# Reordering the queues of a pipelined cross-covariance attention: exponentials ahead of the V copy, doubling ahead of the output matmuls

## The chip, the cores and the metric

One NeuronCore of one Trainium2 chip. The metric is device time in microseconds (us) of the whole kernel; medians are over 3 to 7 runs, and smaller is better. A profile's span is about 1.8 us shorter than the time of the same run (153.7 against 155.51 before).

## The reference

For each of 8x12 heads, with 512 rows of 64 values:

```python
Q_norm = Q / (norm(Q, axis=-2) + 1e-10)          # each of the 64 columns over the 512 rows
K_norm = K / (norm(K, axis=-2) + 1e-10)
attn = einsum('bhnd,bhne->bhde', Q_norm, K_norm)  # 64 x 64 a head
attn = softmax(attn, axis=-1)
out  = einsum('bhnd,bhde->bhne', V, attn)
```

All arrays are float32. Q, K, V and the output are 12.58 MB each, 50.3 MB in all.

## The kernel before

A unit is four heads; there are 24 units. Each head has 32 partitions with 16 rows a partition. Work is spread over steps, so that in step s the Gram matrices of unit s run beside the output matmuls of unit s-3. The order of calls below is the order of instructions in every engine's queue.

```python
def grams(u):                       # TensorE, 64 matmuls
    for t in range(R):              # R = 16
        for h in range(HU):         # HU = 4
            x = qkb[u][NV * h:NV * (h + 1), t, :]      # 32 partitions x (Q 64 | K 64), bf16
            nc.tensor.matmul(gbuf[:, h, 0:2 * D], x, x, start=(t == 0), stop=(t == R - 1), tile_position=(NV * h, 0))
# keep_kq: ScalarE copies K'Q out of the Gram tile; norms: VectorE takes its diagonal, GpSimd ^-0.5
# scale_k: VectorE; logits: TensorE transposes K'Q, 4 f32 matmuls, 8 in the trace; scale_q: VectorE
def exps(u):
    nc.scalar.activation(ex[u], sl[u], AF.Exp)
# normalise: VectorE, sum, reciprocal, product to bf16, rows 0-63 of a
def vtrans(u):                      # TensorE, 8 transposes, then ScalarE
    for t in range(TP):
        nc.tensor.transpose(ps[:, t, :], vb[u][:, t, :], identb)
    nc.scalar.copy(vt[u], ps)

def outs(u, u2):                    # u = s-3, u2 = s-2
    p0 = half(0)                    # TensorE, 16 matmuls
    keep(0, p0)                     # ScalarE copies to so
    p1 = half(1)
    # doubling: rows 0-63 of a, to rows 64-127, by way of PSUM
    nc.tensor.matmul(dup[D:], identb[0:D, 0:D], a2[0:D, :, 0, :], tile_position=(0, D))
    nc.scalar.copy(a2[D:, :, 1, :], dup[D:])
    keep(1, p1)

ltile = ps_l.tile([128, 2, HU, D], F32, name="lgdup")   # one PSUM tile for both
lg, dup = ltile[0:D, 0], ltile[:, 1]
# ... cuts ...
for s in range(U + 3):
    on(load_qk, s + LOAD_AHEAD); on(load_v, s + V_AHEAD); on(store, s - STORE_LAG)
    on(exps, s - 2)
    on(cast_v, s - 2); on(cast_q, s + 1); on(normalise, s - 2); on(scale_k, s - 1)
    on(grams, s); on(keep_kq, s); on(norms, s); on(cast_k, s + 1)
    outs(s - 3, s - 2)
    on(logits, s - 1); on(scale_q, s - 1); on(vtrans, s - 2)
```

## Time and profile before

| | before |
|---|---|
| time, median of the first 3 runs | 153.58 us (152.27 to 154.35) |
| span of the profiled run | 153.7 us (its time 155.51, about 1% above the median) |
| mean granted TensorE clock | 0.769 |
| first and last V cast (vb) on ScalarE | 16.79 and 144.26 us |
| step (kq copy to kq copy) at full / low clock (granted 1.00 and 0.61 in these two) | 5.03 / 5.87 us |

Main rows are shown in the prediction below. A line of the timeline: start, duration, engine, what, and in brackets the idle time before it and its cause.

```profile
q8 instruction: 21, 0.34, 0.9%
```

```profile
PEld L150 <- issue: 6.6, 16, 1.4
```

### The profile page before, as it was taken

Reading aid. Unit: us, or ns where it says so; the run is one execution under the profiler, and the core shown is the slowest. Engines: PE = TensorE matmul, PEld = TensorE weight load, DVE = VectorE, ACT = ScalarE, POOL = GpSimd, SP = SyncE. Lnnn points to the kernel's source line nnn. Section 1 sums busy time; section 2 is a strip of 40 time slices with the busy share of each in tenths; the row PEclk is TensorE's granted clock in tenths of the full one; section 3 lists DMA queues with packets and bytes.
Section 4 is the critical chain, followed back from the end, with each engine's and each line's share of the span. In section 5 each row is a group of like instructions: output and inputs, shape, how many; then the busy total and the mean of one; then the engine's idle time right before and its main releaser. Section 6 shows DMA issues by size and latency. Waiting matters only on the chain.

```text
span 153.7 us, 6358 instructions
## 1 busy us (share of the span) xinstructions
PE 106.8 (69%) x2712; PEld 85.8 (56%) x2712; DVE 95.5 (62%) x360; ACT 101.0 (66%) x169; POOL 43.8 (29%) x35
## 2 busy tenths in 40 slices
PE   0437498768896668759659876958879975947640
PEld 0436386557675557538548754837666853825430
DVE  0378567776767865975876687576686597353300
ACT  3002465985777686796777588567768579677770
POOL 6043045035224405304422512430431531320000
PEclk9999999995569776895985589596855599585555
DMA  4999999999999999999999999999985703321333
GB/s 190 321 402 417 410 408 406 403 414 407 417 411 413 416 410 417 410 415 417 408 419 411 418 419 410 421 413 378 390 320 189 270 4 136 141 82 59 136 136 136
DMA packets 13851, 50.73 MB, mean 330 GB/s; under 512 B 1536, under 2 KB 1536, under 8 KB 13824
## 3 DMA queue, kind: packets, MB, share of 16 engines
q1 hardware_dynamic: 13824, 50.34, 82.5%
q8 instruction: 21, 0.34, 0.9%
q14 instruction: 6, 0.05, 0.1%
HBM read 37.75 MB, written 12.58 MB: 327 GB/s over the span
## 4 chain that ended last, share of the span: by engine, by line
PE 38%; ACT 33%; issue 14%; DMA 8%; SPq 2%; DVE 1%; ACTq 1%
PE lgdup L116 14%; PE vps L138 12%; ACT vb L81 8%; DMA vf<-in_V_dram 8%; ACT so L157 8%; PE gram L88 7%; ACT ab L168 6%; ACT kq L93 5%; PE po L150 4%; ACT ex L124 4%; ACT vt L140 3%; SPq L63 1%; SPq L62 1%; PE lgdup L167 1%; DVE ab L132 1%
## 5 line engine op out<-in xcount | busy, mean ns | idle before, releaser
L105 POOL TENSOR_TENSOR rq<-nsq,mhalf 128x4 f32<-128x4 f32 x24 | 41.4, 1725 | 93.0 <-DVE nsq L100 93.0
L88 PE MATMUL gram<-qkb 32*128 32x128 bf16 x1536 | 40.1, 282 | 9.4 <-DVE qkb L77 9.4
L140 ACT COPY vt<-vps 128x1024 bf16<-128x1024 bf16 x24 | 24.3, 1012 | 29.6 <-PE vps L138 29.6
L88 PEld LDWEIGHTS <-qkb 32*128 32x128 bf16 x1536 | 34.6, 127 | 13.3 <-DVE qkb L77 9.8
L116 PE MATMUL lgdup<-ident,kqs 64*64 64x64 f32 x192 | 22.0, 276 | 19.8 <-ACT ab L168 19.8
L116 PEld LDWEIGHTS lgdup<-ident,kqs 64*64 64x64 f32 x192 | 17.9, 179 | 30.1 <-ACT ab L168 29.9
L157 ACT COPY so<-po 128x512 f32<-128x512 f32 x48 | 28.0, 585 | 1.8 <-PE po L150 0.7
L128 DVE TENSOR_REDUCE esum<-ex 64x4 f32<-64x256 f32 x24 | 9.9, 411 | 28.0 <-ACT ex L124 28.0
L81 ACT CAST vb<-vf 128x1024 bf16<-128x1024 f32 x24 | 24.8, 1032 | 1.8 <-DMA vf<-in_V_dram 1.8
L150 PE MATMUL po<-ab,vt 128*32 128x128 bf16 x768 | 20.4, 259 | 7.9 <-ACT vt L140 4.1
L100 DVE CUSTOM_DVE_ANT_0 scr<-gram,ident 128x128 f32<-128x128 f32 x96 | 22.2, 287 | 3.1 <-ACT kq L93 2.5
L150 PEld LDWEIGHTS <-vt 128*32 128x32 bf16 x768 | 14.8, 116 | 13.2 <-issue 6.6
L138 PE MATMUL vps<-identb,vb 128*128 128x128 bf16 x192 | 21.5, 280 | 0.0
L74 DVE CAST qkb<-qf 128x1024 bf16<-128x1024 f32 x24 | 16.3, 677 | 6.6 <-DMA qf<-in_Q_dram 6.6
L138 PEld LDWEIGHTS <-vb 128*128 128x128 bf16 x192 | 16.0, 127 | 2.9 <-ACT vb L81 0.6
L77 DVE CAST qkb<-kf 128x1024 bf16<-128x1024 f32 x24 | 16.5, 689 | 0.5 <-DMA kf<-in_K_dram 0.5
L120 DVE TENSOR_TENSOR sl<-lgdup,rq 64x256 f32<-64x256 f32 x24 | 10.0, 417 | 9.2 <-PE lgdup L116 9.0
L93 ACT COPY kq<-gram 64x256 f32<-64x256 f32 x24 | 8.8, 367 | 10.4 <-PE gram L88 9.8
L124 ACT ACTIVATE ex<-sl 64x256 f32<-64x256 f32 x24 | 10.0, 415 | 1.9 <-DVE sl L120 1.9
L167 PE MATMUL lgdup<-ab,identb 64*64 64x256 bf16 x24 | 7.5, 314 | 5.1 <-DVE ab L132 4.7
L110 DVE TENSOR_TENSOR kqs<-kq,rq 64x256 f32<-64x256 f32 x24 | 10.1, 423 | 0.8
L132 DVE TENSOR_TENSOR ab<-ex,rinv 64x256 bf16<-64x256 f32 x24 | 10.0, 417 | 0.8
(14 smaller groups left out, 27.5 us busy)
## 6 DMA issues: line engine op xcount, KB each, us to landing
qf<-in_Q_dram SPq DMA_DIRECT2D x24, 512.0 KB, 10.1
kf<-in_K_dram SPq DMA_DIRECT2D x24, 512.0 KB, 10.0
vf<-in_V_dram SPq DMA_DIRECT2D x24, 512.0 KB, 10.1
out_dram<-so SPq DMA_DIRECT2D x24, 512.0 KB, 9.9
```

The source lines that it names most:

```text
L74: nc.vector.tensor_copy(qkb[u][:, :, 0:D], qf[u])
L77: nc.vector.tensor_copy(qkb[u][:, :, D:], kf[u])
L81: nc.scalar.copy(w.rearrange("p t d -> p (t d)"), vf[u])
L88: nc.tensor.matmul(gbuf[:, h, 0:2 * D], x, x, start=(t == 0), stop=(t == R - 1), tile_position=(NV * h, 0))
L93: nc.scalar.copy(kq[u][D:], gbuf[D:, :, 0:D])
L100: nc.vector.tensor_tensor_reduce(out=scr, in0=gbuf[:, h, 0:2 * D], in1=ident, scale=1.0, scalar=1e-20, op0=ALU.mult, op1=ALU.add, accum_ou ...
L105: nc.gpsimd.tensor_tensor(out=r, in0=n2, in1=mhalf, op=ALU.pow)
L116: nc.tensor.matmul(lg[:, h, :], kqs[u][D:, h, :], ident[D:, D:], tile_position=(D, 0))
L138: nc.tensor.transpose(ps[:, t, :], vb[u][:, t, :], identb)
L140: nc.scalar.copy(w, ps)
L150: nc.tensor.matmul(po[rows, k, :], vt[u][:, TP // 2 * i + k, rows], a[:, h].rearrange("p a d -> p (a d)"), tile_position=(0, NV * h),)
L157: nc.scalar.copy(so[u][:, TP // 2 * i:TP // 2 * (i + 1), :], po)
```

## The change

Intent: ScalarE takes the exponentials while TensorE transposes V, rather than after copying the transposed V, and the doubling copy goes ahead of the output copies, so that the logits, which waited 29.9 us for that copy in the profile before, wait less.

```diff
-    def outs(u, u2):
-        def half(i): ...
-        def keep(i, po): ...
-        if 0 <= u < U:
-            p0 = half(0); keep(0, p0); p1 = half(1)
-        if 0 <= u2 < U:
-            nc.tensor.matmul(dup[D:], identb[0:D, 0:D], a2[0:D, :, 0, :], tile_position=(0, D))
-            nc.scalar.copy(a2[D:, :, 1, :], dup[D:])
-        if 0 <= u < U:
-            keep(1, p1)
+    def doubled(u):
+        nc.tensor.matmul(dup[D:], identb[0:D, 0:D], a[0:D, :, 0, :], tile_position=(0, D))
+        nc.scalar.copy(a[D:, :, 1, :], dup[D:])
+    def outs(u):
+        for i in range(2): ...            # 16 matmuls, then the copy to so
@@ the loop over steps
-        on(exps, s - 2)
         on(cast_v, s - 2)
@@
-        outs(s - 3, s - 2)
+        on(doubled, s - 2)
+        on(outs, s - 3)
         on(logits, s - 1)
         on(scale_q, s - 1)
+        on(exps, s - 1)
         on(vtrans, s - 2)
```

(Shortened; the statements on each side are the same, in another order.)

## The prediction

> **What bounds the kernel now.** I read the page's busy shares and DMA row first, then the waits, then the timeline of two whole steps. The kernel runs 27 pipelined steps over 24 units of four heads; step s works on the Gram matrices of unit s, the logits of s-1, the softmax, doubling and V transposes of s-2, and the output matmuls of s-3.

> ```profile
> PE 106.8 (69%) x2712; PEld 85.8 (56%) x2712; DVE 95.5 (62%) x360; ACT 101.0 (66%) x169; POOL 43.8 (29%) x35
> DMA  4999999999999999999999999999985703321333
> ```

> No engine is full. The DMA row is full for the first three quarters, which looks like a memory bound but is not: it is the loads running ahead. The waits say so:

> ```profile
> PEld lgdup L116 <- ACT ab L168: 29.9, 23, 2.2
> ACT vt L140 <- PE vps L138: 29.6, 23, 2.2
> DVE esum L128 <- ACT ex L124: 28.0, 23, 1.9
> ACT vb L81 <- DMA vf<-in_V_dram: 1.8, 1, 1.8
> ```

> After the first unit no compute engine waits for V. Instead, 23 times each, the logits matmuls wait for ScalarE's doubling copy, ScalarE then waits for the V transposes, and VectorE waits for the exponentials: a ring. One turn at full TensorE clock, from one keep of kq to the next:

> ```profile
> 62.34 0.37 ACT L93 COPY kq<-gram 64x256 f32<-64x256 f32 x1
> 62.74 0.59 ACT L157 COPY so<-po 128x512 f32<-128x512 f32 x1
> 62.97 0.29 DVE L100 CUSTOM_DVE_ANT_0 scr<-gram,ident 128x128 f32<-128x128 f32 x1
> 63.35 0.37 ACT L168 CAST ab<-lgdup 64x256 bf16<-64x256 f32 x1
> 63.77 0.68 PE L116 MATMUL lgdup<-ident,kqs 64*64 64x64 f32 x8 [0.95 <-ACT ab L168]
> 63.82 0.69 DVE L77 CAST qkb<-kf 128x1024 bf16<-128x1024 f32 x1
> 64.37 0.62 PE L138 MATMUL vps<-identb,vb 128*128 128x128 bf16 x8
> 64.55 0.42 DVE L120 TENSOR_TENSOR sl<-lgdup,rq 64x256 f32<-64x256 f32 x1
> 65.08 1.01 ACT L140 COPY vt<-vps 128x1024 bf16<-128x1024 bf16 x1 [0.76 <-PE vps L138]
> 65.99 0.41 ACT L124 ACTIVATE ex<-sl 64x256 f32<-64x256 f32 x1
> 66.31 1.03 ACT L81 CAST vb<-vf 128x1024 bf16<-128x1024 f32 x1
> 67.37 0.37 ACT L93 COPY kq<-gram 64x256 f32<-64x256 f32 x1
> ```

> Start to start: kq 0.40, first so 0.61, ab to logits 0.42, logits 0.60, transposes to vt 0.71, vt 0.91, ex 0.32, vb 1.06: 5.03 us. Note that sl is done at 64.97 and ex starts only at 65.99. At the low clock the same ring takes 5.87 us (the kq copies at 78.05 and 83.92), with TensorE as follows:

> ```profile
> 83.30 1.05 PE L150 MATMUL po<-ab,vt 128*32 128x128 bf16 x32
> 84.28 0.42 PE L167 MATMUL lgdup<-ab,identb 64*64 64x256 bf16 x1
> 85.34 1.11 PE L116 MATMUL lgdup<-ident,kqs 64*64 64x64 f32 x8 [0.65 <-ACT ab L168]
> 86.39 1.04 PE L138 MATMUL vps<-identb,vb 128*128 128x128 bf16 x8
> 87.36 1.89 PE L88 MATMUL gram<-qkb 32*128 32x128 bf16 x64
> 89.17 0.79 PE L150 MATMUL po<-ab,vt 128*32 128x128 bf16 x32
> ```

> [...] ex had its input 1.02 us early and sat behind vt. [...] logits (in the bank's lower half) start 0.05 us after the doubling copy of its upper half ends, and in the step at 18 us, where VectorE was free, the norms start 0.03 us after kq ends, though both only read the Gram tile. [...] its clock row reads 9 in the first 30 us, where logits take the slow 1.11 us, so I go by durations. [...] The trace has one table load, 1.28 us, in the whole run, with copies and Exp alternating; their new order adds none.

> **The change part by part.** No instruction is added or removed; counts and shapes stay. Only queue order moves.

> a) Doubling ahead of the outputs. ScalarE's order becomes vb, kq, ab, so, so, ex, vt. The first so leaves the stretch between kq and ab: 0.61 us off the way to the logits, both clocks.

> b) Exponentials ahead of vt. ScalarE no longer waits for the transposes with nothing to do but runs ex in that gap; ex no longer waits for vt, so the softmax of VectorE starts earlier. VectorE's 28.0 us of waiting for ex should nearly vanish.

> c) The new ring. With K the start of kq: ab may start at K+0.39, logits at about K+0.80, done K+1.45 at full clock. VectorE[...] starts the norms at K+0.40; they take 0.85 (62.97 to 63.82), the K cast 0.73 (63.82 to 64.55), so sl starts at K+1.98, after the logits. Then sl to ex 0.44 (14.08 to 14.52 in the first unit, where ex waited for sl alone), ex 0.32, vt 0.91, vb 1.06. Sum 0.40+0.85+0.73+0.44+0.32+0.91+1.06 = 4.71 us. The transposes end at K+2.1 and vt starts at K+2.74, so they are hidden; both so copies end at about K+2.0, before ex at K+2.42. ScalarE's own work, start to start, is 0.91+0.32+1.06+0.39+0.39+0.61+0.60 = 4.28, so it would still idle 0.4. The normalised attention is ready at about K+4.1, the doubling matmul and the outputs end by K+5.0, that is 0.3 into the next step, before its logits at 0.8. So full-clock step: 4.71 against 5.03.

> d) At the low clock, TensorE itself: logits 1.05, transposes 0.97, Gram 1.81 (all start to start above), outputs 0.98 (83.30 to 84.28), doubling an estimated 0.4: 5.2 us. Its idle 0.65 goes, because ab is now copied while the outputs run. So low-clock step: 5.2 against 5.87.

> e) Mix. The timeline puts the first vb at 16.8 and the last at 144.3, 23 steps, 5.54 us each. The profiled time is 155.5 for a span of 153.7, 1.8 more, so the timed 153.58 is a span of 151.8 and a step of (151.8-16.8-9.4)/23 = 5.46, with 9.4 us from the last vb to the end. That is half way between 5.03 and 5.87: half of the steps slow. Keeping half: (4.71+5.2)/2 = 4.96 us. The beginning waits for loads and the final vb-to-store tail has the same ScalarE queue, so both stay. Span 16.8+23x4.96+9.4 = 140.3, time 142.

> **Rivals.** *Transfers take over.* V of unit u is preceded by 8+3u transfers, later four a step. The rows give 413 GB/s, so 1.27 us for 0.524 MB: V of unit 20 lands at 16.8+6x3.8+14x5.1 = 111 us. My vb of unit 20 is at 16.8+20x4.96 = 116, so loads stay 5 us ahead. Were every step at full clock, it would be 111: the loads meet compute, and the time is at best about 136 (16.8+23x4.71+9.4+1.8). For it: the full DMA row. Against: loads now lead by several steps.
> *TensorE takes over altogether.* A denser TensorE could spend all its steps at the slow clock: 16.8+23x5.2+9.4+1.8 = 147.6. For it: 93% busy from 80 to 90 us at clock 0.52. [...]
> *A new wait takes the place.* The doubling matmul, now ahead of the outputs, needs VectorE's attention; if that came late it would block outputs, so copies and logits behind it. Against: I find about 0.5 us of slack (outputs ending at 0.3, logits due at 0.8). Were a quarter to half of the gain lost so, 145 to 148.

> **Range and chances.** The prediction is 142 us, 7.5% less. The range 137.5 to 146.5 runs from nearly all steps at the full clock to nearly all at the slow one, or a lost third. Over 2% faster needs under 150.5: even the slow-clock rival and the half-lost gain pass, so 0.95; within 2% 0.04; slower 0.01, since nothing is added.

> **What would show it right or wrong.** Right: between kq copies 4.7 us where transposes take 0.62, 5.2 where they take 1.04; ex starting 0.03 us after sl; vt starting straight after ex; VectorE's wait for ex and TensorE's wait for ab each under a third; VectorE's norms starting on kq's end. Engine busy times should be unchanged but for TensorE's clock. Wrong: V loads named as what vb waits for (transfers); doubling matmul waiting long for ab from VectorE, with so copies waiting for po (the new wait); slow durations in nearly every step (clock).

The marked cuts are statements on the hardware that no trace here shows. Part c's norms at K+0.40 rest on the one step at 18 us in which they started 0.03 us after kq ended. What "full" and "low" clock stand for, in the profile before: transposes of 0.62 us in the step from 62.34 us, at a granted clock of 1.00, and of 1.04 us at 86.39, in a stretch (80 to 90 us) at 0.52.

## More of the kernel before

TensorE has 64 Gram, 32 output, 8 logits, 8 transposing and 1 doubling matmuls a step, each with a weight load: 226 instructions.

```profile
57.34 0.24 PE L150 MATMUL po<-ab,vt 128*32 128x128 bf16 x4 [1.16 <-issue]
```

The queue that the profile names "instruction" moved 0.34 MB in 21 packets, 16 KB each: the program's own instructions come by DMA. TensorE once stood for 1.16 us in the middle of the output matmuls, waiting for no semaphore that the profile shows ("issue").

## The result, and the profile after

The changed kernel takes 146.46 us (median of 4 runs, 145.65 to 147.19) against 153.77 us for the one before in its 4 runs. The ratio is 0.9537 (95% interval 0.9452 to 0.9623). Ratios here are the mean time of one kernel's fast runs over that of the other's fast runs of the same rounds, so not quite the ratio of the medians. That is faster by 4.6%, where 7.5% was predicted: the direction and the ring were right, the size was not.

First the page's busy and DMA rows, then waits (total us, times, longest).

```profile
PE 105.3 (73%) x2712; PEld 83.4 (58%) x2712; DVE 93.1 (64%) x360; ACT 99.0 (68%) x169; POOL 38.9 (27%) x35
DMA  4999999999999999999999999999999963312333
```

```profile
DVE scr L100 <- ACT kq L93: 22.6, 23, 2.2
PEld L88 <- issue: 12.3, 18, 2.2
PE gram L88 <- issue: 8.9, 9, 2.0
PEld lgdup L116 <- ACT ab L146: 4.0, 7, 0.8
DVE esum L128 <- ACT ex L124: 1.4, 3, 0.5
```

VectorE's wait for the exponentials fell from 28.0 to 1.4 us and the weight load's wait for the doubling copy from 29.9 to 4.0, as intended. The norms now wait for the kq copy, as the new ring has it. ScalarE still loads its table once, for 1.28 us. But the matmuls and weight loads of the Gram matrices now stand idle for "issue", which names no engine.

A full-clock step of the timeline (granted clock 1.00), to hold against the one in the prediction:

```profile
63.26 0.37 ACT L93 COPY kq<-gram 64x256 f32<-64x256 f32 x1
63.66 0.29 DVE L100 CUSTOM_DVE_ANT_0 scr<-gram,ident 128x128 f32<-128x128 f32 x1 [0.68 <-ACT kq L93]
64.51 0.69 DVE L77 CAST qkb<-kf 128x1024 bf16<-128x1024 f32 x1
65.11 0.41 DVE L120 TENSOR_TENSOR sl<-lgdup,rq 64x256 f32<-64x256 f32 x1
65.56 0.42 ACT L124 ACTIVATE ex<-sl 64x256 f32<-64x256 f32 x1 [0.56 <-DVE sl L120]
65.88 0.99 ACT L140 COPY vt<-vps 128x1024 bf16<-128x1024 bf16 x1
66.77 1.04 ACT L81 CAST vb<-vf 128x1024 bf16<-128x1024 f32 x1
67.84 0.37 ACT L93 COPY kq<-gram 64x256 f32<-64x256 f32 x1
```

Start to start: 0.40 + 0.85 + 0.60 + 0.45 + 0.32 + 0.89 + 1.07 = 4.58 us. It is the predicted ring, link by link; ex starts 0.04 us after sl ends and vt follows it at once.

A stretch at low clock (granted 0.50) after the loads had ended (no stall in it, TensorE only):

```profile
121.86 1.05 PE L156 MATMUL po<-ab,vt 128*32 128x128 bf16 x32
122.83 1.11 PE L116 MATMUL lgdup<-ident,kqs 64*64 64x64 f32 x8
123.88 1.03 PE L138 MATMUL vps<-identb,vb 128*128 128x128 bf16 x8
124.85 1.89 PE L88 MATMUL gram<-qkb 32*128 32x128 bf16 x64
126.67 0.42 PE L145 MATMUL lgdup<-ab,identb 64*64 64x256 bf16 x1
127.02 1.05 PE L156 MATMUL po<-ab,vt 128*32 128x128 bf16 x32
```

127.02 - 121.86 = 5.16 us, with TensorE never idle: the 5.2 of the prediction.

So 4.58 and 5.16 both came out as predicted, or better. Yet 14 steps in the loaded stage (kq of unit 5 at 30.44 us to unit 19 at 106.67) took 5.445 us each, more than either. The profile names no wait for it, only these stalls:

```profile
66.19 0.96 PE L88 MATMUL gram<-qkb 32*128 32x128 bf16 x56 [0.64 <-issue]
72.35 0.79 PE L88 MATMUL gram<-qkb 32*128 32x128 bf16 x42 [2.01 <-issue]
78.37 0.93 PE L88 MATMUL gram<-qkb 32*128 32x128 bf16 x27 [1.24 <-issue]
```

(A stall of 0.24 us, ending at 84.39, is left out here.)

```profile
90.41 0.63 PE L156 MATMUL po<-ab,vt 128*32 128x128 bf16 x31 [1.28 <-issue]
96.70 0.44 PE L156 MATMUL po<-ab,vt 128*32 128x128 bf16 x17 [1.46 <-issue]
```

Two things give them away. They end every 6.0 to 6.3 us (66.19, 72.35, 78.37, 84.39, 90.41, 96.70), at different places of the program. And the counts between two of them are nearly fixed, as a view of one stretch shows. Its columns are the length, then the busy time of TensorE's matmuls, its weight loads, VectorE, ScalarE and GpSimd (instructions in brackets), the granted clock, the share of the DMA engines and GB/s:

```profile
66.20:72.30 6.10, 3.51 (x127) 2.66 (x128) 5.06 (x19) 5.49 (x9) 1.43 (x1) 1.00 1.03 413
```

TensorE ran 127 + 128 = 255 instructions, with one of the 226-instruction steps ending inside. The granted clock was 1.00 here, so a low clock does not explain these 6.10 us. Counted from end to end of these six stalls, it ran 256, 256, 257, 259 and 258 matmuls and weight loads, at granted clocks from 0.52 to 1.00. So I take the instructions to come in blocks of 256. The queue fits: its packets have 16 KB each, and they start at 63.6, 69.9, 75.9, 82.0 and 88.0 us, some 2.5 us ahead of the ends of the stalls (66.19 to 90.41). The n-th packet started when TensorE had run about 256 x n instructions (272 at the first, 2706 at the tenth). That these are TensorE's blocks shows in their number: it has 24 x 226 = 5424 instructions, 21 whole blocks of 256; with 218 a step the queue has 20 packets, with 162 it has 15, with 154 it has 14, each time the whole blocks in TensorE's count.

Where the 9.1 us between the two spans (153.7, 144.6) came from, as differences of the same marks: the first vb 2.1 us earlier (16.79 to 14.72), first vb to kq of unit 5 1.2, the 14 loaded steps 2.2, kq of unit 19 to the last vb 3.5, the end 0.1. Only 2.2 us of it comes from 14 of the steps. The first mark is mostly luck of the start: in the versions below, the split one aside, it lies anywhere from 15.0 to 17.6. The profile before is of a run about 1% slow, at nearly the same clock (0.769, against 0.767), so I lean on step lengths and not on the difference of the spans.

### The profile page after: what moved, and what is told of

Read it like the earlier page. It is cut to its first block, busy times and chain, and to the rows that moved or that the text cites. A ratio compares the mean times of both kernels' runs of the same rounds, so it can differ in the third digit from the quotient of the medians.

```text
span 144.6 us, 6358 instructions
## 1 busy us (share of the span) xinstructions
PE 105.3 (73%) x2712; PEld 83.4 (58%) x2712; DVE 93.1 (64%) x360; ACT 99.0 (68%) x169; POOL 38.9 (27%) x35
## 4 chain that ended last, share of the span: by engine, by line
PE 56%; DVE 14%; issue 14%; ACT 9%; DMA 3%; ACTq 0%; SPq 0%; DVEq 0%
PE gram L88 23%; PE lgdup L116 11%; PE po L156 10%; PE vps L138 9%; DVE scr L100 6%; PE lgdup L145 4%; DVE qkb L77 4%; DMA kf<-in_K_dram 3%; ACT vb L81 3%; ACT kq L93 2%; ACT vt L140 2%; DVE sl L120 1%; DVE qkb L74 1%; ACT so L160 1%; DVE ab L132 1%
## 5 line engine op out<-in xcount | busy, mean ns | idle before, releaser
L105 POOL TENSOR_TENSOR rq<-nsq,mhalf 128x4 f32<-128x4 f32 x24 | 36.5, 1520 | 89.9 <-DVE nsq L100 89.9
L88 PE MATMUL gram<-qkb 32*128 32x128 bf16 x1536 | 39.7, 270 | 18.7 <-DVE qkb L77 9.3
L88 PEld LDWEIGHTS <-qkb 32*128 32x128 bf16 x1536 | 32.4, 121 | 24.2 <-issue 12.3
L100 DVE CUSTOM_DVE_ANT_0 scr<-gram,ident 128x128 f32<-128x128 f32 x96 | 22.2, 288 | 22.7 <-ACT kq L93 22.6
L160 ACT COPY so<-po 128x512 f32<-128x512 f32 x48 | 26.0, 589 | 6.4 <-PE po L156 5.2
L156 PE MATMUL po<-ab,vt 128*32 128x128 bf16 x768 | 21.1, 264 | 7.5 <-issue 6.3
L81 ACT CAST vb<-vf 128x1024 bf16<-128x1024 f32 x24 | 25.1, 1045 | 0.0
L140 ACT COPY vt<-vps 128x1024 bf16<-128x1024 bf16 x24 | 24.0, 1001 | 1.2 <-PE vps L138 0.4
L116 PE MATMUL lgdup<-ident,kqs 64*64 64x64 f32 x192 | 22.3, 279 | 2.6 <-ACT ab L146 2.5
L124 ACT ACTIVATE ex<-sl 64x256 f32<-64x256 f32 x24 | 10.0, 417 | 18.7 <-DVE sl L120 18.7
L116 PEld LDWEIGHTS lgdup<-ident,kqs 64*64 64x64 f32 x192 | 18.4, 184 | 6.7 <-ACT ab L146 4.0
L138 PE MATMUL vps<-identb,vb 128*128 128x128 bf16 x192 | 20.4, 269 | 0.1
L93 ACT COPY kq<-gram 64x256 f32<-64x256 f32 x24 | 8.8, 368 | 14.4 <-PE gram L88 13.9
L77 DVE CAST qkb<-kf 128x1024 bf16<-128x1024 f32 x24 | 16.5, 689 | 0.5 <-DMA kf<-in_K_dram 0.5
L138 PEld LDWEIGHTS <-vb 128*128 128x128 bf16 x192 | 14.8, 121 | 2.7 <-issue 0.6
L120 DVE TENSOR_TENSOR sl<-lgdup,rq 64x256 f32<-64x256 f32 x24 | 9.9, 414 | 9.9 <-PE lgdup L116 8.6
L145 PE MATMUL lgdup<-ab,identb 64*64 64x256 bf16 x24 | 8.2, 342 | 5.7 <-DVE ab L132 5.6
L128 DVE TENSOR_REDUCE esum<-ex 64x4 f32<-64x256 f32 x24 | 9.7, 405 | 1.4 <-ACT ex L124 1.4
```

The source lines that it names most:

```text
L77: nc.vector.tensor_copy(qkb[u][:, :, D:], kf[u])
L81: nc.scalar.copy(w.rearrange("p t d -> p (t d)"), vf[u])
L100: nc.vector.tensor_tensor_reduce(out=scr, in0=gbuf[:, h, 0:2 * D], in1=ident, scale=1.0, scalar=1e-20, op0=ALU.mult, op1=ALU.add, accum_ou ...
L105: nc.gpsimd.tensor_tensor(out=r, in0=n2, in1=mhalf, op=ALU.pow)
L116: nc.tensor.matmul(lg[:, h, :], kqs[u][D:, h, :], ident[D:, D:], tile_position=(D, 0))
L140: nc.scalar.copy(w, ps)
```

## The experiments

All times below are medians of fast runs; the kernel before took 152.37, 153.16 and 153.33 us in the three batches. Every version is correct unless it is said not to be.

### Each half of the change alone

```diff
# exps_only: outs(u, u2) as before
-        on(exps, s - 2)
         on(scale_q, s - 1)
+        on(exps, s - 1)
# dup_only: doubled and outs as after
+        on(exps, s - 2)                # first in the step, as before
-        on(exps, s - 1)
```

> Only the exponentials move; doubling and outputs stay as before. Theory F (TensorE's instructions arrive in blocks of 256 at one block per about 6.15 us while the transfers are full, so a step of 226 instructions takes no less than 226/256 x 6.15 = 5.4 us): the ring without the fetch would be about 4.8 us at full clock, still under 5.4, so the loaded stage stays at 5.4 us a step and only the stage after the loads gains a little less: 147 to 149. Theory C (no fetch limit; the low-clock step is simply 5.6 us of TensorE work): the doubling copy again stands between kq and the logits, TensorE idles again, 150 to 152.

> Only the doubling moves; the exponentials still stand behind the V copy. Ring by the durations of before: 4.45 us at full clock and about 5.2 at low clock, both under 5.4. Theory F: same as the whole change, 145.5 to 148. Theory C: the exponentials still start late, so half of the gain or less, 149 to 151.

Measured: exps_only 150.01 us (ratio 0.9867, interval 0.9774 to 0.9961), dup_only 151.21 (0.9948, 0.9854 to 1.0042). Both totals lie at the edges of C's ranges and above F's, so by the totals this did not go F's way. By stages it did: the loaded steps are 5.445 and 5.509 us, against 5.445 with both moves and 5.605 before. Three different orders, nearly one step. (The profile of dup_only is of its fastest run, 149.67 us at clock 0.821; its other four took 151.03 to 151.25.) They differ where the loads do not press: from unit 19 to 23 5.15 us a step for exps_only, 4.57 for dup_only and 5.08 for both. At full clock a step without a stall is 4.94 us for exps_only and 4.57 for dup_only, so there the doubling move alone already has the 4.58 of both. At low clock the doubling move alone is no faster than the kernel before: its steps without a stall reach 5.92 us (75.71 to 81.63 at clock 0.50) where about 5.2 was expected, against 5.87. The two single moves also started 1.3 to 1.7 us later than the whole change (first vb at 16.41 and 16.03, against 14.72). Neither alone gives the gain; the totals cannot be split into a share for each.

### No loads after the fifth unit

```diff
 def load_qk(u):
+    if u >= 5:
+        qf[u], kf[u] = qf[u - 5], kf[u - 5]
+        return
# likewise load_v; wrong results on purpose; same compute instructions
```

> The changed kernel with Q, K and V loaded for the first five units only and reused for the rest (wrong results on purpose); all compute instructions unchanged. Theory F: with the transfers idle the blocks come fast, the TensorE stalls named issue vanish, steps are 4.6 at full clock and about 5.2 at low clock: 136 to 141, blocks less than 5.7 us apart. Theory C: nothing of TensorE's work changed, 145 to 147.

> The kernel before, likewise with loads for five units only (wrong results on purpose). Theory F: its own ring of 5.03 and 5.87 us is mostly slower than the fetch, so it gains little, 0 to 3 us: 151 to 154, and the distance between the two kernels without loads is 11 us or more in place of 7. Theory C: both unchanged, distance 7 us.

Measured: the changed kernel 133.43 us (ratio 0.8787, 0.8718 to 0.8856), the kernel before 149.56 (0.9845, 0.9749 to 0.9940), below its expected 151. Rival C falls: no TensorE work changed, and 13 us went. The reordering is worth 149.56 - 133.43 = 16.1 us without loads, and 7 with them. The DMA row of the changed kernel without loads:

```profile
DMA  4999995404422430342244044213403421432133
```

The instruction counts are those of the page after (2712 matmuls and as many weight loads), and the DMA engines are at less than half from about 27 us on. No matmul stalls on "issue" any more, blocks come unevenly and mostly sooner (4.3 to 7.5 us apart, 5.3 on average, where less than 5.7 was expected of all), and the loaded-stage step is 4.582, the ring exactly. This is better than predicted (136 to 141), and the mean granted clock was 0.877 in place of 0.767. In the new order the versions without stalls have the higher clock (0.844 to 0.877 in their profiles, against 0.767). The old order without loads has no stall over 0.25 us either, and its fast runs stay at 0.771 to 0.776, so there the clock did not rise without stalls; what raises it was not tested apart.

### Fewer TensorE instructions, all loads kept

```diff
# after_gram256: wrong results on purpose, the same number of columns streamed
-        for t in range(R):
+        for t in range(0, R, 2):
-                nc.tensor.matmul(gbuf[:, h, 0:2 * D], x, x, ...)
+                y = qkb[u][NV * h:NV * (h + 1), t:t + 2, :].rearrange("p a d -> p (a d)")
+                nc.tensor.matmul(gbuf[:, h, 0:4 * D], x, y, ...)
# after_k64: correct; each head on 64 partitions for Q and K
+    Q2, K2 = (... "(u g p f) -> u p g f", p=128, g=2 ...)
-                x = qkb[u][NV * h:NV * (h + 1), t, :]                   # 16 x 4 matmuls of 32 rows
+                x = qkb[u][D * q:D * (q + 1), R // 2 * g + t, :]        # 8 x 2 x 2 matmuls of 64 rows
# after_bf16lg: correct
-        kqs: F32, transposed against ident
+        kqs: BF16, transposed against identb          # 16 instructions become 8
```

> The changed kernel, all loads kept, but the Gram matmuls taken in pairs: 32 of 256 columns in place of 64 of 128 (same columns streamed, cross terms wrong on purpose), so TensorE has 162 instructions a step in place of 226. Theory F: 162/256 x 6.15 = 3.9 us, no longer a bound; the ring's 4.6 us and the full transfers (5.1 us a step) are: 134 to 140, no TensorE stalls named issue over 0.5 us. Rival T (loads slow the engines in some other way, say by memory contention, and the number of instructions does not matter): 144 to 147.

> A correct kernel with as few TensorE instructions as the one above: Q and K are laid out with 64 partitions a head (two rows of 2 KB a partition), so a Gram matrix takes 8 matmuls of 64 rows in place of 16 of 32 rows, 162 instructions a step. Theory F: 134 to 141, if 2 KB rows do not slow the transfers. Rival T: 144 to 148.

> The changed kernel with the logits' transposing matmuls in bf16: 4 matmuls and 4 weight loads a step in place of 8 and 8, 218 instructions a step. Theory F: 218/256 x 6.15 = 5.24 us a step in the loaded stage in place of 5.43, some 16 steps: 3 us less, 143 to 145. Rival T: shorter TensorE work at the low clock only, 145 to 147.

Measured: after_gram256 135.86 us (ratio 0.8895, 0.8816 to 0.8973), after_k64 138.60 (0.9093, 0.9004 to 0.9182), after_bf16lg 141.21 (0.9282, 0.9180 to 0.9384). Rival T falls: the loads are all there, the DMA row stays full, and yet 8 to 11 us go with the 64 instructions, and 5 with eight. The step of the loaded stage fits the count: 218 instructions give 5.227 us, where 218/256 x 6.15 is 5.24. By time, after_bf16lg did 2 us better than expected. The 14 loaded steps gave 14 x (5.445 - 5.227) = 3.1 us, as expected; most of the rest came after them, from the kq copy of unit 19 to the last vb (26.1 us in place of 28.6), which the expectation left out.

At 162 instructions another bound shows. The DMA row and a wait of after_k64:

```profile
DMA  4999999999999999999999999999999999984233
```

```profile
ACT vb L83 <- DMA vf<-in_V_dram: 5.7, 9, 2.0
```

The engines keep to 4.58 us a step until about 67 us, then wait for V and take 5.1: at last the loads themselves. This is the rival "transfers take over" of the prediction, with the 5.1 us a step that it worked out; its best time for that, about 136 us, is near the 135.86 and 138.60 measured.

### The layout under the old order, and the instructions put back

```diff
# before_k64: the layout of after_k64 in the kernel before
# after_k64_tiny: after_k64 with 32 matmuls of one column ahead of each unit's Gram sums
+        for i in range(8):
+            for g in range(2):
+                for q in range(2):
+                    x = qkb[u][D * q:D * (q + 1), R // 2 * g + i, :]
+                    nc.tensor.matmul(gbuf[:, 2 * g + q, 511:512], x, x[:, 0:1], start=True, stop=True, ...)
```

> The kernel before with the 64-partition layout, 162 TensorE instructions a step. Theory F: the fetch no longer binds, but its own ring of 5.03 and 5.87 us does, so it gains no more than it did without loads: 149 to 151, and the change of order is worth 10 to 13 us at this instruction count in place of 7 at 226. If the layout itself were what is faster, it would gain as much as the changed kernel did (8 us): 145 to 146.

> The 64-partition version with 32 matmuls of one column added ahead of the Gram sums (results not used), so 226 TensorE instructions a step again with little work in them. Theory F: the loaded stage goes back to 226/256 x 6.15 = 5.4 us a step with stalls named issue: 143 to 148. If the work and not the number counts: 32 short matmuls fit into TensorE's idle time at full clock, 138 to 141.

Measured: before_k64 147.54 us (ratio 0.9605, 0.9528 to 0.9682), after_k64_tiny 150.03 (0.9773, 0.9696 to 0.9850).

The old order gains some 6 us from the layout, more than the 2 to 4 expected, and not quite the 8 of the changed kernel. Its steps are its own ring, 5.03 and 5.87 (in the profile of a slow run, 151.78 us), with no stall over 0.3 us. So the old order lost to the fetch too. But it gains more than without any loads (ratio 0.9605 against 0.9845), so part of the gain is not the fetch; what else gives it was not tested. At 162 instructions the change is worth 147.54 - 138.60 = 8.9 us, under the 10 to 13 expected; the loads cap the changed kernel there.

Putting the instructions back brings the stalls back:

```profile
PE gram L96 <- issue: 4.3, 4, 1.9
PE po L164 <- issue: 5.2, 4, 2.3
```

The loaded step is 5.414 us, again that of 226 instructions. The total is 2 us above what was expected, because the added matmuls also cost TensorE some 0.42 us a step at full clock (56.95 to 57.37 us of its profile, where the transposes take 0.62), which is felt once the loads end: 5.5 us a step there. So this run shows the step of the loaded stage, and not a clean price of the number alone.

### Shorter transfers

```diff
-        nc.sync.dma_start(out=vf[u], in_=Vf[u])
+        for i in range(2):
+            nc.sync.dma_start(out=vf[u][64 * i:64 * (i + 1)], in_=Vf[u][64 * i:64 * (i + 1)])
# after_split: likewise Q, K and the output
```

> The changed kernel with each 512 KB transfer issued as two of 64 partitions (rows of 4 KB as before). [...] blocks less than 6 us apart in the loaded stage, 138 to 145. If its wait does not depend on the packets: blocks 6.0 to 6.3 us apart, 145 to 148.

This was meant to test whether a block's wait depends on the length of the data packets. The first range above is for a wait that does, the second for one that does not. Measured: 182.56 us (ratio 1.1964, 1.1803 to 1.2124), outside both expectations. The page's GB/s row shows why:

```profile
GB/s 122 232 228 231 228 231 232 231 233 239 240 243 248 283 303 346 340 327 342 320 268 344 351 342 275 320 254 313 313 287 324 325 330 352 337 326 340 307 186 116
```

Transfers of 64 partitions moved 231 GB/s in the first third where those of 128 moved some 410, so the kernel waited for V (34.4 us in 16 waits). Instruction blocks came 8.4 to 8.9 us apart there. Nor did the edit shorten what the profile calls packets: it counts 12288 packets of 4 KB of data in both versions, only fewer of them to a transfer. So the run does not tell what sets the 6.15 us; that stays open.

### Both count reductions

> The 64-partition version with bf16 logits matmuls, 154 instructions a step, correct. Ring (4.6 us) and transfers (5.1 us a step in the second half) bind, not the fetch: no more than 1.5 us off, 137 to 139.

Measured: 137.58 us (ratio 0.8958, 0.8909 to 0.9006), correct, as expected: 154 instructions in place of 162 bring 1 us at most, since the loads bind. It is the fastest correct version, 10% below the kernel before.

| version | instr. a step | time | loaded step | unit 19 to 23, a step |
|---|---|---|---|---|
| before | 226 | 153.77 | 5.605 | 5.640 |
| after | 226 | 146.46 | 5.445 | 5.080 |
| exps_only | 226 | 150.01 | 5.445 | 5.145 |
| dup_only | 226 | 151.21 | 5.509 | 4.572 |
| after_k64_tiny | 226 | 150.03 | 5.414 | 5.505 |
| after_bf16lg | 218 | 141.21 | 5.227 | 4.850 |
| after_k64 | 162 | 138.60 | 4.929 | 4.960 |
| after_gram256 (wrong result) | 162 | 135.86 | 4.700 | 4.892 |
| after_noload (wrong result) | 226 | 133.43 | 4.582 | 4.578 |

Loaded step is the mean of 14, from the kq copy of unit 5 to that of unit 19, in the profile.

## Why the prediction was right or wrong

- What bounds the kernel before: half right. The ring was there, with its 5.03 and 5.87 us. But "The DMA row ... looks like a memory bound but is not" stopped a step early. The full DMA row does not delay V (one wait, of 1.8 us); it delays TensorE's own instructions, whose blocks came 6.15 us apart in the changed kernel with all loads, and 5.3 on average without. The kernel before stood at 5.6 us a step, only 3% above the 5.43 that the fetch allows.
- Parts a, b and c, the new ring: right. It is 4.58 where 4.71 was predicted. The term that was off is the K cast, read as 0.73 from a step in which sl had to wait for the logits; its real pitch is 0.60.
- Part d, the low-clock step of 5.2: right where nothing stalls (5.16).
- Part e, the mix, is the step that failed: "(4.71+5.2)/2 = 4.96 us". It takes each step as the larger of ring and TensorE work, and leaves out a term, the supply of instructions, 5.43 us in the loaded stage at 226 instructions. The runs show it there (5.41 to 5.51 in four versions), gone without loads (4.58), and lower with the count (5.23 at 218). Over 23 steps the mean was (135.22-14.72)/23 = 5.24, not 4.96, 6.4 us more; the early start gave 2.1 back. All of the excess is in the loaded stage: its 14 steps took 5.445 us, the other nine (135.22-14.72-14x5.445)/9 = 4.92.
- The share of slow steps, kept at half: with the fetch in the way the mean clock stayed as it was (0.769 before, 0.767 after). Without loads it was 0.877 in the new order and 0.771 to 0.776 in the old one; what sets it was not shown.
- The rivals: "Transfers take over" had the right culprit by the wrong path, until the instruction count was lowered; then V was waited for, at its 5.1 us a step. "A new wait takes the place" was what happened, though not at the doubling matmul: the new wait is one that no row names except as "issue".
- Of the signs, those of the ring came (waits for ex and ab under a third, ex behind sl, norms behind kq), and they could not warn of the missing term. The first sign, steps of 4.7 or 5.2 us, failed: ten of the 14 loaded steps took over 5.3 us. That is where the missing term shows.

## What to carry to other kernels

This is one kernel, so it is a check to make and not a law. Where a fully unrolled kernel gives one engine hundreds of short instructions a step while the DMA queues are full, count them: instructions a step, over the 256 of a block counted here, times the spacing of the instruction-queue packets (6.15 us) gave 5.43 us, a floor here: the three reorderings took 5.445, 5.445 and 5.509. Look for idle time put down to "issue" that recurs at a fixed number of instructions (256 to 259 here) rather than at a fixed line. Fewer and larger matmuls (here 64 rows in place of 32) paid about as much as the better order, some 6 us alone against 7, and 15 with it.
